# A two-layer trunk with attention woven into its projections: TensorE held in program order, VectorE released

## Chip, cores and metric

The kernel runs on one core of a Trainium2 chip. The metric is device time in microseconds. Before the change three runs took 2830.03, 2831.26 and 2836.04 us; the median is 2831.26 us.

## What is computed

A stream `x` of 2048 frames by 1024 channels passes two layers. All data are float32.

```python
# layer 0 (mixer A)
h = rms_norm(x, a_norm);  u, z = split(h @ a_w_in)
pooled = trailing_means(u, windows 2, 4, 8, 16 by channel group) - u
x = x + ((pooled @ w_group) * a_scale * silu(z)) @ a_w_out
x = x + (p[0] @ ple_w[0]) * sigmoid(x @ ple_gate_w[0])
# shared keys and values
k, v = split(rms_norm(x, kv_norm) @ w_kv);  k = rms_norm(k per head)
# layer 1 (mixer B)
q, z = split(rms_norm(x, b_norm) @ b_w_in);  q = rms_norm(q per head)
A[t,s] = beta[t,s] * prod_{s<j<t} (1 - beta[t,j]),  beta = sigmoid(q.k / 8)   # 16 heads of 64, s < t
x = x + ((A @ v) * silu(z)) @ b_w_out
x = x + (p[1] @ ple_w[1]) * sigmoid(x @ ple_gate_w[1])
```

## The kernel before

**Tiling.** The stream is cut into four chunks of 512 frames. Channels lie on the 128 partitions, eight tiles per chunk. Each float32 operand of a matmul is held as a high and a low part (a cast on ACT, then a subtraction on DVE or POOL: `split`, `put_split`), and each product is made of three matmuls, hi.hi, hi.lo, lo.hi, 128 x 128 by 512 columns. A dense output tile is 24 matmuls into one of two `psd` banks.

**Dense work** is one long generator, `stream()`. `first_part(s)` makes layer 0 for chunk s (`mixer`, `out_steps`, `gate_steps`), the gate z, and the first eight heads' q, k, v (`kvq(s, kind, 0)`); `second_part(s)` the other eight heads' q, k, v; `post(c)` is layer 1 behind attention. Each `yield` is one matmul. `marks` notes which halves are done: mark (1, 0) is `first_part(1)`.

**Weights** come through `plan`, `pump`, `unit` and `take`: nine tiles `wpair` of 512 KB turn round. In chunk 0 a unit is loaded raw (256 KB), split and written back (`once`); later it is loaded from there. A `kvq` product takes eight units and gives each back in its fourth row block (`j == 3`), so the next kind's units are loaded while the current kind ends. The weights of layer 1 behind attention (`b_w_out`, `gate_b`, `ple_b`) are split beforehand by `keep`, 36 pieces, one after each 36th dense step (`kraw`, `kp`).

**Attention** walks over 160 slots (chunk c of queries, head h, chunk kc of keys, from kc = c down to 0), four steps per slot. In step n the program issues `turn` for the step five earlier (up to four transposes of `pp` into a `psa` bank, L748; a cast to `at` on ACT, L751; a subtraction on DVE, L754), `front` (two logit matmuls into a `psl` bank, L728 and L729; a sigmoid on ACT, L731; a `TENSOR_TENSOR_SCAN` on DVE that forms the product along the keys, L736), half of the dense share (`fill`), `gather` for the step seven earlier (two output matmuls, L761 and L762), and the other half. `rate` sets the dense share: about 27 matmuls a step in chunk 0, 13 in chunk 1, 7 in chunks 2 and 3. `psa` has two banks, which the transposes of finished q and k rows (`keyed.finish`, `pst`, L552) and the norm helpers also use.

**Order.** The compiler schedules the whole program from a model of its times and may reorder each engine's instructions. `tc.keep_in_program_order` keeps the instructions so marked in the order of the program, against each other, on their engine. Before, that holds for the scans (L736) and the subtractions of `turn` (L754) on DVE, and in chunks 2 and 3 for one of six matmuls of a dense product (L225, `state["pin"]`). Everything else on TensorE is placed by the model.

**Scratch.** Finished keys and queries go to DRAM by pairs of heads, one tile `[128, 2, 512]` per pair; `load_k` reads a head's high and low rows in two DMAs, `load_q` in four.

Of the kernel before, what the change touches and what calls it, by code (L numbers as in the profile page):

```python
# [15 lines left out]
P = 128  # L16
# [3 lines left out]
NH = 16  # L20
# [16 lines left out]
def trunk_kernel(ctx, tc, x, p, a_norm, wu_t, wz_a, w_group, a_scale, a_w_out, kv_norm, w_kv,  # L37
                 k_norm, b_norm, b_w_q, b_w_z, b_q_norm, b_w_out, ple_a, ple_b, gate_a, gate_b, out):
    nc = tc.nc
    V, A, G, T = nc.vector, nc.scalar, nc.gpsimd, nc.tensor  # L40

# [32 lines left out]
    od = [[scratch(f"od{s}_{o}", [P, 2, W5]) for o in range(KT)] for s in range(NSUB)]  # L74
    qd = [[scratch(f"qd{s}_{m}", [P, 2, W5]) for m in range(NH // 2)] for s in range(NSUB)]
    kd = [[scratch(f"kd{s}_{m}", [P, 2, W5]) for m in range(NH // 2)] for s in range(NSUB)]
    vd = [[scratch(f"vd{s}_{b}", [8, P, 4, P]) for b in range(2)] for s in range(NSUB)]
# [18 lines left out]
    att = lambda nm: pool.tile([P, 2, W5], F32R, tag="at", name=nm, bufs=3)  # L96

    state = {"solo": True, "pin": False, "turn": 0, "lo": 0}

# [119 lines left out]
    def product(ps, us, acts, c0, back):  # L219
        n = len(acts)  # L220
        i = 0
        for u, kts in us:
            for e, kt in enumerate(kts):
                hi, lo = (u[:, l, e, c0 : c0 + P] for l in range(2))
                ins = T.matmul(ps, hi, acts[kt][:, 0], start=(i == 0), stop=False)  # L225
                if state["pin"] and e == 0:
                    tc.keep_in_program_order(ins)
                yield
                T.matmul(ps, hi, acts[kt][:, 1], start=False, stop=False)  # L229
                yield  # L230
                i += 1
                T.matmul(ps, lo, acts[kt][:, 0], start=False, stop=(i == n))  # L232
                if back and e == len(kts) - 1:
                    give_back()
                yield
# [251 lines left out]
    def kvq(s, kind, b):  # L487
        ck = chunk[s]
        us = take(KT)
        for j in range(4):  # L490
            tk = slice(j * P, (j + 1) * P)
            ps = dense()
            for kt in range(KT):
                u = us[kt][0]
                for xh, wh in ((0, 0), (1, 0), (0, 1)):
                    T.matmul(ps, ck["x2"][kt][:, xh, tk], u[:, wh, 0], start=(kt == 0 and xh == wh),  # L496
                             stop=(kt == KT - 1 and wh == 1))
# [35 lines left out]
    def keyed(s, kind, b, j, ps, rj):  # L533
# [15 lines left out]
        def finish(m):  # L549
# [37 lines left out]
    def gate_z(s):  # L587
# [105 lines left out]
    def load_q(c, h):  # L693
        qa, qb = qryt("qa"), qryt("qb")
        rows = qd[c][h // 2][h % 2 * HD : (h % 2 + 1) * HD]
        for l in range(2):
            nc.sync.dma_start(out=f(qa)[l * HD : (l + 1) * HD], in_=rows[:, l])
            nc.sync.dma_start(out=f(qb)[(1 - l) * HD : (2 - l) * HD], in_=rows[:, l])
        return qa, qb

    def load_k(kc, h):
        kk = keyt("kk")
        rows = kd[kc][h // 2][h % 2 * HD : (h % 2 + 1) * HD]
# [18 lines left out]
    def front(st, j):  # L722
# [10 lines left out]
        def scan():  # L733
            least = floor[:, r0:][:, ::-1] if st["diag"] else floor[:, 0:1].to_broadcast([P, w])
            tc.keep_in_program_order(
                V.tensor_tensor_scan(out=pp[:, r0:][:, ::-1], data0=pp[:, r0:][:, ::-1], data1=least,  # L736
                                     initial=1.0 if st["diag"] else st["carry"][j], op0=ALU.mult, op1=ALU.max))
            st["carry"][j] = pp[:, r0 : r0 + 1]
# [4 lines left out]
    def turn(st, kt):  # L743
        j0 = kt if st["diag"] else 0
        pt = bank("psa", "psa")
        for j in range(j0, 4):
# [5 lines left out]
        st["at"][kt] = at  # L752
        return lambda: tc.keep_in_program_order(
            V.tensor_tensor(out=at[:, 1, cs], in0=pt[:, cs], in1=f(at[:, 0, cs]), op=ALU.subtract))  # L754

# [82 lines left out]
    def fill(share):  # L838
        nonlocal owed, count
        owed += share  # L840
        while owed >= 1.0:
            next(run, None)
            owed -= 1.0
            count += 1
            if count % 36 == 0 and kept:
                keep(*kept.pop(0))

    scan = None
    for n in range(4 * len(slots) + LAG_G):
# [5 lines left out]
        if i < len(slots):  # L855
            state["pin"] = slots[i][0] >= NSUB - 2
            if j == 0 and i + 1 < len(slots):
# [15 lines left out]
    for _ in run:  # L873
        pass
    state["solo"], state["pin"] = True, False
    for _ in post(NSUB - 1):
# [65 lines left out]
```

## Time and profile before

| | |
|---|---|
| median of three runs | 2831.26 us |
| the profiled execution's own time | 2833.48 us |
| its span | 2831.7 us |
| mean granted TensorE clock | 0.986 |
| DMA, whole span | 643.43 MB, mean 227 GB/s |

Busy time counts an instruction from its start to its modelled end; matmuls overlap, so the distance from one start to the next is what a matmul takes of TensorE's time. A wait is named by the instruction that waited and the one that released it. The span starts with 354 us without attention: layer 0 and the first half of q, k, v of chunk 0. Attention of chunk 0 lasts to about 708 us, of chunk 1 to about 1416 us. From some 2760 us on only `post` of the last chunk is left.

### The profile page before, as it was taken

Reading aid. Unit: us, or ns where it says so; the run is one execution under the profiler, and the core shown is the slowest. Engines: PE = TensorE matmul, PEld = TensorE weight load, DVE = VectorE, ACT = ScalarE, POOL = GpSimd, SP = SyncE. Lnnn points to the kernel's source line nnn. Section 1 sums busy time; section 2 is a strip of 40 time slices with the busy share of each in tenths; the row PEclk is TensorE's granted clock in tenths of the full one; section 3 lists DMA queues with packets and bytes.
Section 4 is the critical chain, followed back from the end, with each engine's and each line's share of the span. In section 5 each row is a group of like instructions: output and inputs, shape, how many; then the busy total and the mean of one; then the engine's idle time right before and its main releaser. Section 6 shows DMA issues by size and latency. Waiting matters only on the chain.

```text
span 2831.7 us, 38727 instructions
## 1 busy us (share of the span) xinstructions
PE 2729.6 (96%) x13400; PEld 2250.0 (79%) x13400; DVE 1832.6 (65%) x2369; ACT 1275.0 (45%) x2496; POOL 873.3 (31%) x699
## 2 busy tenths in 40 slices
PE   7999989989999999999999999989999999999999
PEld 7888867867888888888877887868877888887767
DVE  5645446747344776655568978657667777767772
ACT  4435543445344345444444555444444444444441
POOL 1354533546533244442322434211221101111002
PEclk8999999999999999999999999999999999999999
DMA  5647899979887845668775454676586768666535
GB/s 212 223 142 277 318 340 355 325 218 302 293 289 278 255 142 174 196 226 272 254 242 163 142 158 152 225 262 206 159 276 192 249 207 263 208 194 225 169 121 185
DMA packets 300496, 643.43 MB, mean 227 GB/s; under 512 B 51206, under 2 KB 83974, under 8 KB 300300
## 3 DMA queue, kind: packets, MB, share of 16 engines
q1 hardware_dynamic: 298716, 639.63, 68.6%
q8 instruction: 106, 1.74, 0.2%
q10 hardware_dynamic: 1584, 1.33, 0.2%
q14 instruction: 90, 0.74, 0.1%
HBM read 471.43 MB, written 161.02 MB: 223 GB/s over the span
## 4 chain that ended last, share of the span: by engine, by line
PE 78%; DMA 8%; DVE 7%; ACT 2%; issue 2%; POOL 1%; SPq 1%; ACTq 0%; DVEq 0%; POOLq 0%
PE psd L496 15%; PE psd L225 11%; PE psd L229 11%; PE psd L232 11%; PE psa L748 7%; PE pso L762 4%; PE psl L729 4%; PE psl L728 3%; PE pso L761 3%; DVE pp L736 3%; PE psd L251 2%; PE psd L248 2%; PE psd L246 2%; DMA wpair<-once 2%; DVE at L754 1%
## 5 line engine op out<-in xcount | busy, mean ns | idle before, releaser
L736 DVE TENSOR_TENSOR_SCAN pp<-pp,floor 128x512 f32<-128x512 f32 (+3 forms) x640 | 779.0, 1219 | 5.2 <-ACT pp L731 4.6
L496 PE MATMUL psd<-wpair,x 128*128 128x512 f32 x2304 | 582.9, 395 | 10.0 <-ACT wpair L137 3.9
L754 DVE TENSOR_TENSOR at<-psa,at 128x512 fp32r<-128x512 f32 (+3 forms) x640 | 378.7, 595 | 312.9 <-ACT at L751 311.1
L496 PEld LDWEIGHTS psd<-wpair,x 128*128 128x128 f32 x2304 | 425.4, 189 | 98.6 <-ACT wpair L137 5.8
L751 ACT CAST at<-psa 128x512 fp32r<-128x512 f32 (+3 forms) x640 | 330.9, 523 | 378.3 <-PE psa L748 358.7
L731 ACT ACTIVATE pp<-psl 128x512 f32<-128x512 f32 (+3 forms) x640 | 333.4, 535 | 305.8 <-PE psl L729 194.8
L748 PE MATMUL psa<-ident,pp 128*128 128x128 f32 x2176 | 357.4, 276 | 45.0 <-DVE at L754 23.7
L748 PEld LDWEIGHTS psa<-ident,pp 128*128 128x128 f32 x2176 | 272.9, 141 | 132.0 <-DVE at L754 38.7
L762 PE MATMUL pso<-at,vv 128*128 128x512 f32 (+3 forms) x640 | 275.1, 430 | 0.6 <-DVE at L754 0.6
L728 PE MATMUL psl<-kk,qa 128*128 128x512 f32 (+3 forms) x640 | 244.3, 382 | 13.2 <-DMA kk<-kd 9.8
L761 PE MATMUL pso<-at,vv 128*128 128x512 f32 (+3 forms) x640 | 238.7, 374 | 7.6 <-DMA once<-kp 5.4
L729 PE MATMUL psl<-kk,qb 128*128 128x512 f32 (+3 forms) x640 | 236.0, 370 | 0.0
L225 PE MATMUL psd<-x,wpair 128*128 128x512 f32 x592 | 233.5, 394 | 0.0
L232 PE MATMUL psd<-x,wpair 128*128 128x512 f32 x592 | 232.5, 393 | 0.0
L229 PE MATMUL psd<-x,wpair 128*128 128x512 f32 x592 | 232.5, 393 | 0.0
L225 PE MATMUL psd<-xp,wpair 128*128 128x512 f32 x512 | 203.5, 398 | 0.5 <-DMA wpair<-once 0.5
L229 PE MATMUL psd<-xp,wpair 128*128 128x512 f32 x512 | 201.7, 394 | 0.0
L232 PE MATMUL psd<-xp,wpair 128*128 128x512 f32 x512 | 201.2, 394 | 0.0
L133 POOL TENSOR_TENSOR wpair<-wraw,wpair 128x512 fp32r<-128x512 f32 x98 | 139.0, 1423 | 153.6 <-ACT wpair L131 152.5
L728 PEld LDWEIGHTS psl<-kk,qa 128*128 128x128 f32 x640 | 122.8, 192 | 40.8 <-ACT pp L731 11.2
L465 POOL TENSOR_TENSOR xj<-x 128x512 f32<-128x512 f32 x64 | 106.9, 1675 | 139.6 <-DVE sg L476 131.9
L761 PEld LDWEIGHTS pso<-at,vv 128*128 128x128 f32 x640 | 122.0, 191 | 27.7 <-ACT at L751 11.0
(162 smaller groups left out, 4621.0 us busy)
## 6 DMA issues: line engine op xcount, KB each, us to landing
wpair<-once SPq DMA_DIRECT2D x384, 512.0 KB
once<-wpair SPq DMA_DIRECT2D x80, 512.0 KB
kk<-kd SPq DMA_DIRECT2D x320, 128.0 KB
vv<-vd SPq DMA_DIRECT2D x160, 256.0 KB
wpair<-wf SPq DMA_DIRECT2D x48, 512.0 KB
once<-kp SPq DMA_DIRECT2D x36, 512.0 KB
wraw<-in_a_w_out_dram SPq DMA_DIRECT2D x64, 256.0 KB
wraw<-in_gate_a_dram SPq DMA_DIRECT2D x64, 256.0 KB
```

Of the source, the lines that this page charges most:

```text
L225: ins = T.matmul(ps, hi, acts[kt][:, 0], start=(i == 0), stop=False)
L229: T.matmul(ps, hi, acts[kt][:, 1], start=False, stop=False)
L232: T.matmul(ps, lo, acts[kt][:, 0], start=False, stop=(i == n))
L496: T.matmul(ps, ck["x2"][kt][:, xh, tk], u[:, wh, 0], start=(kt == 0 and xh == wh), stop=(kt == KT - 1 and wh == 1))
L728: T.matmul(ps[:, :w], qa[:, qs], kk[:, :w], start=True, stop=False)
L729: T.matmul(ps[:, :w], qb[:, qs], kk[:, :w], start=False, stop=True)
L731: A.activation(out=pp[:, r0:], in_=ps[:, :w], func=AF.Sigmoid, scale=-1.0)
L736: V.tensor_tensor_scan(out=pp[:, r0:][:, ::-1], data0=pp[:, r0:][:, ::-1], data1=least, initial=1.0 if st["diag"] else st["carry"][j], op0 ...
L748: T.transpose(pt[:, j * P : (j + 1) * P], pp[:, r0 + kt * P : r0 + (kt + 1) * P], ident)
L754: V.tensor_tensor(out=at[:, 1, cs], in0=pt[:, cs], in1=f(at[:, 0, cs]), op=ALU.subtract))
L761: T.matmul(po[:, cs], vv[:, kt, :], at[:, 0, cs], start=(st["diag"] and kt == 0), stop=False)
L762: T.matmul(po[:, cs], vv[:, kt, :], at[:, 1, cs], start=False, stop=(st["last"] and kt == 3))
```

## The change

- Every matmul and transpose goes through a small class `T`. While `state["hold"]` is set, each is marked `keep_in_program_order`. `hold` is set when mark (0, 0) is reached, just ahead of the first attention slot, and cleared ahead of the last `post`. The pin on L225 goes.
- The scans and the subtractions of `turn` on DVE are no longer marked.
- `qd` and `kd` are stored by head, `[2, 64, 512]`: two stores per finished tile instead of one; `load_k` is one DMA instead of two, `load_q` three instead of four.
- `keep` starts only when mark (1, 0) is set.
- 60 dense matmuls instead of 24 go between the loads of the first slot and its first step.
- In `kvq`, the token norm `r2`, where it isn't there yet, comes after the first product instead of after three quarters of it. In `gate_z`, the broadcast of `r2` comes at step 20 of a product instead of 9.

```diff
-    V, A, G, T = nc.vector, nc.scalar, nc.gpsimd, nc.tensor
+    V, A, G = nc.vector, nc.scalar, nc.gpsimd
+    state = {"solo": True, "hold": False, "turn": 0, "lo": 0}
+
+    class T:
+        @staticmethod
+        def matmul(*a, **k):
+            return held_in_order(nc.tensor.matmul(*a, **k))
...
+    def held_in_order(ins):
+        return tc.keep_in_program_order(ins) if state["hold"] else ins
...
-    kd = [[scratch(f"kd{s}_{m}", [P, 2, W5]) for m in range(NH // 2)] for s in range(NSUB)]
+    kd = [[scratch(f"kd{s}_{h}", [2, HD, W5]) for h in range(NH)] for s in range(NSUB)]
...
-                ins = T.matmul(ps, hi, acts[kt][:, 0], start=(i == 0), stop=False)
-                if state["pin"] and e == 0:
-                    tc.keep_in_program_order(ins)
+                T.matmul(ps, hi, acts[kt][:, 0], start=(i == 0), stop=False)
...
-                if j == 0 and kt == 5 and "r2" not in ck:
-                    ck["r2"] = token_norm(ck["acc2"], "y")
...
+            if "r2" not in ck:
+                ck["r2"] = token_norm(ck["acc2"], "y")
...
-            nc.sync.dma_start(out=(kd if kind == "k" else qd)[s][4 * b + m], in_=f(hl))
+            for e in range(2):
+                nc.sync.dma_start(out=(kd if kind == "k" else qd)[s][8 * b + 2 * m + e].rearrange("l d n -> d l n"),
+                                  in_=f(hl)[e * HD : (e + 1) * HD])
...
-                    if first and o == 2 and i == 9:
+                    if first and o == 2 and i == 20:
...
-        for l in range(2):
-            nc.sync.dma_start(out=f(kk)[l * HD : (l + 1) * HD], in_=rows[:, l])
+        nc.sync.dma_start(out=f(kk), in_=kd[kc][h].rearrange("l d n -> (l d) n"))
...
-            tc.keep_in_program_order(
-                V.tensor_tensor_scan(out=pp[:, r0:][:, ::-1], data0=pp[:, r0:][:, ::-1], data1=least,
-                                     initial=1.0 if st["diag"] else st["carry"][j], op0=ALU.mult, op1=ALU.max))
+            V.tensor_tensor_scan(out=pp[:, r0:][:, ::-1], data0=pp[:, r0:][:, ::-1], data1=least,
+                                 initial=1.0 if st["diag"] else st["carry"][j], op0=ALU.mult, op1=ALU.max)
...
-        return lambda: tc.keep_in_program_order(
-            V.tensor_tensor(out=at[:, 1, cs], in0=pt[:, cs], in1=f(at[:, 0, cs]), op=ALU.subtract))
+        return lambda: V.tensor_tensor(out=at[:, 1, cs], in0=pt[:, cs], in1=f(at[:, 0, cs]), op=ALU.subtract)
...
-    state["solo"] = False
+    state["solo"], state["hold"] = False, True
...
-    for _ in range(24):
+    for _ in range(60):
...
-            if count % 36 == 0 and kept:
+            if count % 36 == 0 and kept and (1, 0) in marks:
```

All of TensorE's matmuls now have line 46 and its transposes line 50. The first place to look at is TensorE's order behind the second half of q, k, v of chunk 2, where attention passes from chunk 1 to chunk 2. Before (`psl` are logits, `pso` outputs, `psa` attention's transposes):

```order
L728 MATMUL psl_13973<-kk_13823,qa_13527 128x512
L729 MATMUL psl_13973<-kk_13823,qb_13528 128x512
L761 MATMUL pso_13671<-at_13821,vv_13467 128x512
L728 MATMUL psl_14018<-kk_13823,qa_13527 128x512
L729 MATMUL psl_14018<-kk_13823,qb_13528 128x512
L748 MATMUL psa_13851<-ident_60,pp_13690 128x128
L748 MATMUL psa_13851<-ident_60,pp_13723 128x128
L748 MATMUL psa_13851<-ident_60,pp_13755 128x128
L748 MATMUL psa_13851<-ident_60,pp_13793 128x128
L762 MATMUL pso_13671<-at_13821,vv_13467 128x512
L728 MATMUL psl_14042<-kk_13823,qa_13527 128x512
L729 MATMUL psl_14042<-kk_13823,qb_13528 128x512
```

The same place of the program in the changed kernel, TensorE (`psd` are dense products, `pst` transposes of finished k rows):

```order
L46 MATMUL psl_13698<-kk_13441,qa_13255 128x512
L46 MATMUL psl_13698<-kk_13441,qb_13256 128x512
L46 MATMUL psd_13648<-wpair_13539,x2_11080 128x512
L50 MATMUL pst_13706<-ident_60,qs_13300 128x128
L50 MATMUL pst_13706<-ident_60,qs_13400 128x128
L50 MATMUL pst_13706<-ident_60,qs_13474 128x128
L50 MATMUL pst_13706<-ident_60,qs_13558 128x128
L46 MATMUL psd_13648<-wpair_13544,x2_11187 128x512 x3
L46 MATMUL psd_13648<-wpair_13551,x2_11288 128x512 x3
L46 MATMUL pso_13418<-at_13609,vv_13208 128x512 x2
L46 MATMUL psd_13738<-wpair_13223,x2_10648 128x512 x3
L46 MATMUL psd_13738<-wpair_13503,x2_10674 128x512 x3
```

Three logit pairs stood within twelve instructions and no dense matmul among them; now one logit pair is followed by thirteen dense matmuls, with an output pair between.

The second place is a change from one of the q, k, v weights to the next in chunk 1, TensorE. Before (`wpair_7895`, `_8082`, `_8087`, `_8106` are the new weight's first four units):

```order
L496 MATMUL psd_8146<-wpair_8082,x2_6095 128x512 x3
L496 MATMUL psd_8146<-wpair_8087,x2_6164 128x512 x3
L496 MATMUL psd_8210<-wpair_7895,x2_6069 128x512 x3
L496 MATMUL psd_8210<-wpair_8082,x2_6095 128x512 x3
L496 MATMUL psd_8210<-wpair_8087,x2_6164 128x512 x3
L728 MATMUL psl_8400<-kk_8034,qa_8028 128x384
L729 MATMUL psl_8400<-kk_8034,qb_8029 128x384
L496 MATMUL psd_8146<-wpair_8106,x2_6258 128x512 x3
L496 MATMUL psd_8210<-wpair_8106,x2_6258 128x512 x3
```

The changed kernel at such a place (`wpair_7386`, `_7615`, `_7638`, `_7643` and so on are the units, in the order of the plan):

```order
L46 MATMUL psd_7696<-wpair_7386,x2_5927 128x512 x3
L46 MATMUL psd_7696<-wpair_7615,x2_5969 128x512 x3
L46 MATMUL psd_7696<-wpair_7638,x2_6030 128x512
L50 MATMUL psa_7704<-ident_60,pp_7309 128x128
L50 MATMUL psa_7704<-ident_60,pp_7375 128x128
L50 MATMUL psa_7704<-ident_60,pp_7441 128x128
L50 MATMUL psa_7704<-ident_60,pp_7549 128x128
L46 MATMUL psl_7711<-kk_7304,qa_7299 128x256
L46 MATMUL psl_7711<-kk_7304,qb_7300 128x256
L46 MATMUL psd_7696<-wpair_7638,x2_6030 128x512 x2
L46 MATMUL psd_7696<-wpair_7643,x2_6115 128x512 x3
L46 MATMUL psd_7696<-wpair_7648,x2_6181 128x512 x3
```

Before, a second product (`psd_8210`) was begun on the three units that were there, ahead of the first product's fourth unit; now one product runs through all its units.

More of the change, by code (lines that the diff above doesn't have):

```diff
@@ L39, in trunk_kernel, with transpose @@
     nc = tc.nc
-    V, A, G, T = nc.vector, nc.scalar, nc.gpsimd, nc.tensor
+    V, A, G = nc.vector, nc.scalar, nc.gpsimd
[4 more added lines that the diff above has]
+            return held_in_order(nc.tensor.matmul(*a, **k))
+        @staticmethod
+        def transpose(*a, **k):
+            return held_in_order(nc.tensor.transpose(*a, **k))
+    def held_in_order(ins):
+        return tc.keep_in_program_order(ins) if state["hold"] else ins
     cp = ctx.enter_context(tc.tile_pool(name="cp", bufs=1))
@@ L74, in trunk_kernel @@
     od = [[scratch(f"od{s}_{o}", [P, 2, W5]) for o in range(KT)] for s in range(NSUB)]
-    qd = [[scratch(f"qd{s}_{m}", [P, 2, W5]) for m in range(NH // 2)] for s in range(NSUB)]
-    kd = [[scratch(f"kd{s}_{m}", [P, 2, W5]) for m in range(NH // 2)] for s in range(NSUB)]
+    qd = [[scratch(f"qd{s}_{h}", [2, HD, W5]) for h in range(NH)] for s in range(NSUB)]
+    kd = [[scratch(f"kd{s}_{h}", [2, HD, W5]) for h in range(NH)] for s in range(NSUB)]
     vd = [[scratch(f"vd{s}_{b}", [8, P, 4, P]) for b in range(2)] for s in range(NSUB)]
@@ L96, in trunk_kernel @@
     att = lambda nm: pool.tile([P, 2, W5], F32R, tag="at", name=nm, bufs=3)
-    state = {"solo": True, "pin": False, "turn": 0, "lo": 0}
     def bank(tag, nm):
@@ L694, in load_q @@
         qa, qb = qryt("qa"), qryt("qb")
-        rows = qd[c][h // 2][h % 2 * HD : (h % 2 + 1) * HD]
+        nc.sync.dma_start(out=f(qa), in_=qd[c][h].rearrange("l d n -> (l d) n"))
         for l in range(2):
-            nc.sync.dma_start(out=f(qa)[l * HD : (l + 1) * HD], in_=rows[:, l])
-            nc.sync.dma_start(out=f(qb)[(1 - l) * HD : (2 - l) * HD], in_=rows[:, l])
+            nc.sync.dma_start(out=f(qb)[(1 - l) * HD : (2 - l) * HD], in_=qd[c][h][l])
         return qa, qb
@@ L702, in load_k @@
         kk = keyt("kk")
-        rows = kd[kc][h // 2][h % 2 * HD : (h % 2 + 1) * HD]
-        for l in range(2):
-            nc.sync.dma_start(out=f(kk)[l * HD : (l + 1) * HD], in_=rows[:, l])
+        nc.sync.dma_start(out=f(kk), in_=kd[kc][h].rearrange("l d n -> (l d) n"))
         return kk
@@ L855, in trunk_kernel @@
         if i < len(slots):
-            state["pin"] = slots[i][0] >= NSUB - 2
             if j == 0 and i + 1 < len(slots):
@@ L874, in trunk_kernel @@
         pass
-    state["solo"], state["pin"] = True, False
+    state["solo"], state["hold"] = True, False
     for _ in post(NSUB - 1):
```

## Prediction

> **What bounds the kernel now.** I read the page's first lines, then the busy time by stage, then TensorE's waits, then the timeline at the worst waits.
>
> ```profile
> span 2831.7 us, 38727 instructions
> PE 2729.6 (96%) x13400; PEld 2250.0 (79%) x13400; DVE 1832.6 (65%) x2369; ACT 1275.0 (45%) x2496; POOL 873.3 (31%) x699
> ```
>
> TensorE is the bound; the rest of the span, 102 us, is its idle time. What can be won is idle time, and time at half clock. The stages (columns: stretch, length, busy time of PE, PEld, DVE, ACT, POOL, then granted clock, DMA share, GB/s) say where these lie:
>
> ```profile
> 0.00:354.00 354.00, 339.11 (x1589) 286.56 (x1590) 193.94 (x338) 162.70 (x300) 142.62 (x128) 0.97 0.66 234
> 354.00:708.00 354.00, 323.32 (x1491) 264.04 (x1489) 210.50 (x260) 153.67 (x304) 167.58 (x136) 0.97 0.91 308
> 708.00:1416.00 708.00, 701.85 (x3468) 581.38 (x3467) 416.88 (x541) 316.84 (x633) 279.60 (x226) 1.00 0.73 238
> 1416.00:2620.00 1204.00, 1165.56 (x5901) 959.11 (x5900) 887.52 (x1079) 566.67 (x1116) 259.52 (x193) 0.99 0.65 207
> 2620.00:2832.00 212.00, 199.78 (x957) 158.90 (x956) 123.74 (x153) 75.12 (x144) 24.00 (x17) 0.98 0.50 157
> ```
>
> Idle time plus clock loss (length times one minus the clock) per stage: first, before attention, 14.9 + 10.6, which the change doesn't touch; second, attention of chunk 0, 30.7 + 10.6 = 41 us; third, 6; fourth, 38.4 + 12 = 50; last, 12.2 + 4.2 = 16. So 91 of the removable 113 us lie in the second and fourth. TensorE's waits by cause:
>
> ```profile
> PE psa L748 <- DVE at L754: 23.7, 35, 2.1
> PE psd L281 <- ACT uh L268: 14.7, 2, 7.8
> PE psa L748 <- DVE pp L736: 13.8, 9, 4.5
> PE psl L728 <- DMA kk<-kd: 9.8, 3, 5.3
> PE pso L761 <- DMA once<-kp: 5.4, 1, 5.4
> PE psa L748 <- DVE hl L120: 4.6, 2, 3.4
> PE psd L496 <- ACT wpair L137: 3.9, 4, 1.6
> ```
>
> Nearly all are attention instructions (L748, L728, L761) that wait for something a few us old. The dense matmuls that could have covered them had been put elsewhere. The fourth stage at its start shows it:
>
> ```profile
> 1430.26 0.60 PE L748 MATMUL psa<-ident,pp 128*128 128x128 f32 x4
> 1430.61 0.48 PE L761 MATMUL pso<-at,vv 128*128 128x512 f32 x1
> 1432.16 0.66 PE L552 MATMUL pst<-ident,qs 128*128 128x128 f32 x4 [1.07 <-DVE at L754]
> ...
> 1436.92 0.39 PE L728 MATMUL psl<-kk,qa 128*128 128x512 f32 x1
> 1437.15 0.40 PE L729 MATMUL psl<-kk,qb 128*128 128x512 f32 x1
> 1437.53 0.49 PE L761 MATMUL pso<-at,vv 128*128 128x512 f32 x1
> 1441.45 0.88 PE L748 MATMUL psa<-ident,pp 128*128 128x128 f32 x3 [3.43 <-DVE hl L120]
> 1443.27 0.66 PE L748 MATMUL psa<-ident,pp 128*128 128x128 f32 x2 [0.94 <-DVE at L754]
> ```
>
> From 1430 to 1443 us not one dense matmul (psd) runs: attention and its transposes stand back to back, so a psa bank is asked for again before ScalarE and VectorE have emptied it. (Start to start, a 512-wide matmul takes 1437.15 - 1436.92 = 0.23 us, four transposes 0.35.) In the second stage the cause is different:
>
> ```profile
> 630.26 0.62 ACT L119 CAST ple<-pin 128x512 fp32r<-128x512 f32 x1 [2.53 <-DMA pin<-in_p_dram]
> ...
> 630.91 0.69 DVE L120 TENSOR_TENSOR ple<-pin,ple 128x512 fp32r<-128x512 f32 x1 [2.46 <-ACT ple L119]
> 631.52 1.22 DVE L736 TENSOR_TENSOR_SCAN pp<-pp,floor 128x512 f32<-128x512 f32 x1
> ...
> 632.79 1.11 PE L748 MATMUL psa<-ident,pp 128*128 128x128 f32 x4 [4.52 <-DVE pp L736]
> ...
> 634.34 0.63 PE L229 MATMUL psd<-ple,wpair 128*128 128x512 f32 x1
> 634.77 0.63 PE L232 MATMUL psd<-ple,wpair 128*128 128x512 f32 x1
> ```
>
> A load is late (DMA share 0.91), ACT's cast waits for it, the split on DVE for ACT, the scan stands behind the split, and TensorE behind the scan: 4.52 us. After that the pace is 0.43 us per matmul: half clock. The Trainium skill (TensorE: Matmul & The Clock Gate, "The HAM clock gate") halves the clock after an idle window of about 3.4 us and restores it after a busy one; the 4.52 us wait agrees, and by that rule waits under 3.4 us cost only themselves.
>
> **The change, part by part.**
>
> *TensorE in program order, fourth stage.* A step in program order is four transposes, two logit matmuls, half of the dense share, two output matmuls, the other half. What a transposition's bank needs before reuse, and what the output matmul needs before it starts, is one cast and one subtraction, with at most a scan ahead of them:
>
> ```profile
> L751 ACT CAST at<-psa 128x512 fp32r<-128x512 f32 x448 | 260.7, 587 | 301.1 <-PE psa L748 288.4 <-PE pso L762 7.0 <-DVE at L754 1.5
> L754 DVE TENSOR_TENSOR at<-psa,at 128x512 fp32r<-128x512 f32 x448 | 301.3, 676 | 258.1 <-ACT at L751 257.1
> L736 DVE TENSOR_TENSOR_SCAN pp<-pp,floor 128x512 f32<-128x512 f32 x448 | 620.5, 1386 | 4.9 <-ACT pp L731 4.3
> ```
>
> 0.59 + 0.68 = 1.3 us, with a scan 2.7. I counted in both orders, with the spacings above, how much TensorE work lies in between. psa banks reused within 2.5 us, from chunk 2 up to the last dense-free stretch: 55 before, none now. Output matmuls within 2 us of their transposition, whole kernel: 83 before, 1 now. Stretches over 2 us without a dense matmul: 64 before (247 us), 5 now (49 us, nearly all at the very end). Keys come at least 10 us after their buffer is free (4.5 us before), the very end apart. So the causes L754, hl, L736 and kk go in this stage. VectorE could still be late by itself: its busy share is 887.52/1204 = 0.74. I leave 8 of the 50 us: **-42**; bounds 0 and -50.
>
> *Second stage.* Splitting b weights (36 pieces of 256 KB read, 512 KB written, 28 MB in all) moves behind mark (1, 0), to the third stage, whose DMA share is 0.73. The second stage moved 308 GB/s x 354 us = 109 MB, so it loses up to a quarter of its traffic, and the casts that wait for these loads. That removes the 5.4 us at once<-kp and most waits of the scan kind. Against it: program order takes away what TensorE did at a change of the q, k, v weights. Before, it ran two products in turn on the units already there; now all eight units are needed in a row, 3 x 0.23 = 0.69 us apart. A unit's buffer is free 24 matmuls, 5.5 us, before its successor's turn, with a step's attention (0.35 + 4 x 0.23 = 1.3 us) some 6.7. What landing takes under load (from the chain of waits and the timeline):
>
> ```profile
> 820.52 6.02 DMA wpair<-once
> ...
> 1235.24 9.16 DMA wpair<-once
> ...
> 826.58 0.98 PE L496 MATMUL psd<-wpair,x 128*128 128x512 f32 x3 [1.52 <-DMA wpair<-once]
> ...
> 780.00:830.00 50.00, 48.06 (x246) 39.94 (x245) 24.29 (x35) 21.83 (x45) 19.84 (x17) 1.00 0.85 288
> ```
>
> Unit tiles whose buffer comes free less than 8 us before use: 26 before, 69 now. Seven units of 0.524 MB at 288 GB/s take 12.7 us; the last is due 6.7 + 6 x 0.8 = 11.5 us after the first buffer is free. That is a wait of 1 to 3 us per change. Two changes lie in this stage, and their units still pass through a cast and a split (the 3.9 us at wpair L137), so I take 4 us each, and leave 7 us of the rest: 41 becomes 15, **-26**; bounds +20 and -41.
>
> *Third stage.* Eleven further changes have short leads, six of 6 to 7.5 us and five near 8, and the b weights' traffic now lies here. I take the low end for the six and next to nothing for the five: 6 x 1 + 5 x 0.2 = **+7**; bounds 0 and +33 (11 x 3). The page's best slice moved 355 GB/s; at that rate seven units take 10.3 us. The Trainium skill (DMA: Bandwidth & Descriptors, "Where 436 GB/s comes from") gives the port ceiling as 435 GB/s and HBM's share as about 358: at the ceiling this estimate would be 8.4 us, the waits and this term would vanish and the sum would be 7 us lower. No slice here is above 355.
>
> *The end.* The last attention steps have no dense work in either kernel (30 steps, 43 us of issue in both orders), but the stream runs dry 36 matmuls earlier, since 60 instead of 24 go ahead of attention (36 x 0.23 = 8 us moved, none added). VectorE sets the pace there:
>
> ```profile
> 2683.00:2755.00 72.00, 36.75 (x30) 0.95 0.34 107
> 2683.00:2755.00 72.00, 21.08 (x34) 0.95 0.34 107
> ```
>
> (scans, then subtractions): 1.23 + 0.62 = 1.85 us a step against TensorE's 1.3. In strict order the scan of a slot's last row has as little as 1.7 us of issue before it is read. **+4**; bounds -5 and +16 (30 x 0.55).
>
> *VectorE's order free*: scans and subtractions may now swap with dense work. Bounds: the 13.8 us of scan waits gone, or doubled; both are inside the stage bounds; I take 0, nearest the group's 4.9 us of idle before scans. *Keys and queries by head*: 160 + 64 loads fewer, 64 stores more, all on SP, which nothing on TensorE's list names except kk (9.8 us, counted above): 0; if the two stores came late, the cover is the half chunk between projection and attention. *r2 after the whole product, rb2 at step 20 instead of 9*: 11 x 0.23 = 2.5 us more cover for the chain through POOL: 0.
>
> Sum against the profiled execution: 2833.5 - 42 - 26 + 7 + 4 = 2776.5. That execution is 2.2 us above the median of the runs (2831.3), so 2774, rounded 2775.
>
> **The rivals.**
>
> *VectorE takes over (half the gain).* Where chunk 3's mixer runs beside chunk 2's attention, it is nearly full:
>
> ```profile
> 1558.00:1628.00 70.00, 68.73 (x351) 56.51 (x350) 63.26 (x74) 37.91 (x75) 29.03 (x24) 1.00 0.47 140
> ```
>
> 63.26/70 = 0.90, and yet TensorE lost only 1.3 us in that slice; that speaks against it. If half of the 42 and 26 stays: 2774 + 34 = 2808.
>
> *Slower: the weight changes.* Thirteen changes have the short leads. I charged 15 us. If the seven units arrive later than I think (the 9.16 us landing is the row for it), each change waits 4.5 us and, as at 632.79, runs about 11 matmuls at half pace (11 x 0.2 = 2.2): 13 x 6.7 = 87 us, 2774 + 72 = 2846. It decides from (57 + 15)/13 = 5.5 us a change. Against it: waits of 1.5 us on these weights today, at leads of 6.3 us and more. By the clock rule cited above, waits that stay under 3.4 us leave this case impossible, since 13 x 3.4 = 44.
>
> *No difference.* The compiler's order might not bind, but the printed orders differ as described, so only gains and losses that cancel remain: 2831.
>
> **How the numbers follow.** Forecast 0.62; half the gain 0.22; no difference 0.05; weight changes 0.11. The forecast's own range is 2735 (2831 less all 91 us, and 5 won at the end) to 2798 (a third of the 68 us stays); with the half gain and the 16 us that the end may cost on top of it (2808 + 16), the range is 2735 to 2824. A measurement here tells about 0.2% from no change (5.7 us; the three runs spread over 6). Faster 0.84, same 0.05, slower 0.11.
>
> **What would show it.** Right: the fourth stage's idle time under 10 us, L748's waits for L754 near zero before the last 140 us, the second stage's clock near 1.00. The new waits stand at psd for wpair at the changes of q, k, v, each 1 to 3 us. Wrong: waits over 3.4 us there with a clock under 0.97 between 354 and 1416 us; or L748 still waiting for L754 and L736 in the fourth stage with VectorE over 0.85 busy; or a last stage with over 25 us idle.

## The result and the profile after

The changed kernel takes 2836.6 us (median of 20 runs) where the kernel before takes 2832.5 us on the same chip: ratio 1.0015, 95% interval 1.0008 to 1.0022. That lies inside the 0.2% which count as no difference. The forecast of 2775 us and its range, 2735 to 2824, are missed. The page of the changed kernel begins like this:

```profile
span 2832.9 us, 38130 instructions
...
PE 2733.4 (96%) x13400; PEld 2246.7 (79%) x13400; DVE 1840.4 (65%) x2369; ACT 1271.2 (45%) x2496; POOL 870.4 (31%) x699
```

Span and busy times are within a few us of before. By the page's head, then, nothing happened. The stages say otherwise (columns: stretch, length, busy time of PE, PEld, DVE, ACT, POOL, then granted clock, DMA share, GB/s):

```profile
354.00:708.00 354.00, 327.67 (x1507) 266.61 (x1506) 190.15 (x250) 138.39 (x271) 139.98 (x117) 0.96 0.73 239
708.00:1416.00 708.00, 672.88 (x3241) 546.05 (x3239) 413.03 (x521) 312.77 (x628) 293.91 (x236) 0.98 0.78 259
1416.00:2620.00 1204.00, 1194.04 (x6098) 986.47 (x6097) 913.22 (x1104) 579.57 (x1150) 267.40 (x202) 1.00 0.66 215
2620.00:2833.00 213.00, 198.99 (x975) 160.55 (x973) 130.10 (x158) 78.24 (x150) 27.01 (x19) 0.99 0.49 163
```

By the prediction's measure, idle time plus length times one minus the clock, the stages lose this much in us. (The clock has two digits, which leaves about 2, 4 and 6 us open in the three.)

| | second | third | fourth | last |
|---|---|---|---|---|
| before | 30.7 + 10.6 = 41 | 6 | 38.4 + 12 = 50 | 16 |
| after | 26.3 + 14.2 = 41 | 35.1 + 14.2 = 49 | 10.0 + 0 = 10 | 14.0 + 2.1 = 16 |

The fourth stage gained 40 us, and the third gave 43 back. TensorE's waits in the changed kernel, whole span, and behind them the first of these in the third stage alone (708 to 1416 us):

```profile
PE psd L46 <- DMA wpair<-once: 29.1, 28, 7.2
PE psd L46 <- ACT uh L277: 14.2, 2, 8.1
PE psd L46 <- ACT wpair L148: 13.6, 5, 6.1
PE psd L46 <- DVE xr L449: 7.5, 2, 4.2
PE psa L50 <- DVE pp L743: 6.6, 9, 2.0
PE psa L50 <- DVE at L760: 5.5, 9, 1.2
```

```profile
PE psd L46 <- DMA wpair<-once: 24.0, 24, 7.2
```

The wait of transposes for the subtraction fell from 23.7 to 5.5 us, that for the scan from 13.8 to 6.6. The list is now headed by dense matmuls that wait for weight units, 29.1 us in 28 waits (before, 3.2 us in 3), 24.0 us of them in the third stage. Another 13.6 us (before, 3.9) go to units that ACT still casts; all of these lie in the second stage, the longest 6.1 us. The start of the fourth stage, for comparison with the dense-free stretch of before (timeline of TensorE):

```profile
1430.06 0.60 PE L50 MATMUL psa<-ident,pp 128*128 128x128 f32 x4
1430.41 0.36 PE L46 MATMUL psl<-kk,qa 128*128 128x256 f32 x1
1430.61 0.28 PE L46 MATMUL psl<-kk,qb 128*128 128x256 f32 x1
1430.73 1.53 PE L46 MATMUL psd<-wpair,x 128*128 128x512 f32 x6
1432.10 0.40 PE L46 MATMUL pso<-at,vv 128*128 128x256 f32 x2
1432.33 1.79 PE L46 MATMUL psd<-wpair,x 128*128 128x512 f32 x7
```

Thirteen dense matmuls stand in a step, and nothing waits. What the order costs shows at a change of the q, k, v weights in chunk 1, the one whose order stands ahead of the prediction, first on TensorE and then on SP's queue (start, duration, engine, line, tile, count):

```profile
816.65 0.39 PE L46 MATMUL psd<-wpair,x 128*128 128x512 f32 x1
...
823.20 0.94 PE L46 MATMUL psd<-wpair,x 128*128 128x512 f32 x3
831.34 2.30 PE L46 MATMUL psd<-wpair,x 128*128 128x512 f32 x4 [7.20 <-DMA wpair<-once]
```

```profile
818.17 0.58 SPq L713 DMA_DIRECT2D kk<-kd  x1
...
819.32 3.33 SPq L571 DMA_DIRECT2D kd<-hl  x4
822.75 0.70 SPq L540 DMA_DIRECT2D vd<-vv  x1
823.50 3.36 SPq L523 DMA_DIRECT2D vs<-vr  x2
826.91 0.41 SPq L530 DMA_DIRECT2D ve<-vr  x1
827.43 4.06 SPq L156 DMA_DIRECT2D wpair<-once  x8
```

At 823.20 stand the three matmuls of the new weight's first unit; for the second TensorE waits 7.20 us. The matmul at 816.65 is the first on the old weight's second unit in its last row block, so a buffer was free by then. The loads were not slow to land so much as late to be issued: SP was issuing without a gap from 818 us on, and the units' turn came at 827.43. The stretch in and behind the wait runs at half clock:

```profile
828.00:832.00 4.00, 0.66 (x2) 0.56 (x3) 0.69 (x1) 0.62 (x1) 1.26 (x1) 0.50 0.85 294
```

The Trainium skill (TensorE: Matmul & The Clock Gate, "The HAM clock gate") halves the clock after an idle window of about 3.4 us; a wait of 7.20 us with a clock of 0.50 agrees.

### The profile page after: what moved, and what is told of

Its sections match the earlier page's. It is cut to its first block, busy times and chain, and to the rows that moved or that the text cites. A ratio compares the mean times of both kernels' runs of the same rounds, so it can differ in the third digit from the quotient of the medians.

```text
span 2832.9 us, 38130 instructions
## 1 busy us (share of the span) xinstructions
PE 2733.4 (96%) x13400; PEld 2246.7 (79%) x13400; DVE 1840.4 (65%) x2369; ACT 1271.2 (45%) x2496; POOL 870.4 (31%) x699
## 4 chain that ended last, share of the span: by engine, by line
PE 79%; DMA 8%; DVE 5%; SPq 2%; issue 2%; ACT 2%; POOL 2%; ACTq 0%; DVEq 0%; POOLq 0%
PE psd L46 55%; PE psl L46 8%; PE pso L46 7%; PE psa L50 7%; DMA wpair<-once 3%; DVE pp L743 2%; DVE at L760 1%; DMA wraw<-in_b_w_q_dram 1%; PE pst L50 1%; DMA xin<-in_x_dram 1%; DMA vs<-vr 1%; POOL wpair L144 1%; PE pst L46 1%; SPq L523 1%; DMA kraw<-in_b_w_out_dram 1%
## 5 line engine op out<-in xcount | busy, mean ns | idle before, releaser
L46 PE MATMUL psd<-x,wpair 128*128 128x512 f32 x2304 | 599.3, 393 | 3.5 <-ACT sg L481 3.5
L46 PEld LDWEIGHTS psd<-x,wpair 128*128 128x128 f32 x2304 | 427.0, 188 | 92.5 <-ACT sg L481 4.6
L46 PE MATMUL psd<-xp,wpair 128*128 128x512 f32 x1536 | 391.8, 396 | 6.4 <-DMA wpair<-once 6.4
L46 PE MATMUL pso<-at,vv 128*128 128x512 f32 (+3 forms) x1280 | 361.5, 364 | 0.2 <-DVE at L760 0.2
L46 PEld LDWEIGHTS psd<-xp,wpair 128*128 128x128 f32 x1536 | 287.4, 190 | 66.3 <-DMA wpair<-once 7.7
L46 PEld LDWEIGHTS pso<-at,vv 128*128 128x128 f32 x1280 | 240.7, 189 | 54.0 <-DVE at L760 0.5
L46 PE MATMUL psd<-og,wpair 128*128 128x512 f32 x744 | 202.6, 395 | 2.0 <-DVE os L773 2.0
L46 PE MATMUL psd<-mp,wpair 128*128 128x512 f32 x768 | 196.9, 398 | 7.5 <-DVE xr L449 7.5
L46 PEld LDWEIGHTS psd<-mp,wpair 128*128 128x128 f32 x768 | 145.0, 192 | 38.2 <-DVE xr L449 8.3
L46 PEld LDWEIGHTS psd<-og,wpair 128*128 128x128 f32 x744 | 137.5, 188 | 31.5 <-DVE os L773 2.6
```

Source lines behind the costliest of these rows:

```text
L46: return held_in_order(nc.tensor.matmul(*a, **k))
```

## The experiments

The theory after the result: program order of TensorE does in the fourth stage what was forecast, and loses it again at the weight changes of the second and third stage. Rivals: the new place of the b weights, the storage by head, VectorE's freed order. No kernel below leaves anything out of the computation. Ratios are to the kernel before, with their 95% intervals.

### Program order only from chunk 2 on

```diff
-    state["solo"], state["hold"] = False, True
+    state["solo"] = False
...
         x_ = rate(i)
+        state["hold"] = slots[min(i, len(slots) - 1)][0] >= NSUB - 2
```

> The changed kernel, but TensorE is held in program order only while chunks 2 and 3 attend; chunks 0 and 1 are placed by the compiler as before. Weight-change theory (in chunks 0 and 1 strict order uses up new q, k, v units faster than they land): the fourth stage keeps its gain (idle about 10 us instead of 38) and the second and third lose most of their 43 + 14 us of waits at wpair, so about 2800 us. Queue theory (the two stores per key or query tile hold up SP's queue, whatever TensorE's order): waits at wpair stay, about 2820. Moved-traffic theory (b weights split in the third stage): third stage idle stays above 20 us, about 2820.

Measured: 2805.3 us, ratio 0.9898 (0.9882 to 0.9913).

```profile
354.00:708.00 354.00, 339.00 (x1565) 275.84 (x1564) 196.96 (x260) 142.54 (x282) 149.47 (x121) 0.98 0.75 250
708.00:1416.00 708.00, 687.48 (x3367) 566.74 (x3366) 420.81 (x537) 322.39 (x649) 304.37 (x241) 0.99 0.79 266
1416.00:2620.00 1204.00, 1194.38 (x6093) 988.49 (x6092) 922.42 (x1109) 577.79 (x1144) 261.27 (x195) 0.99 0.65 214
```

The second stage loses 15 + 7 = 22 us instead of 41, the third 20.5 + 7 = 28 instead of 49, and the idle time of the fourth is as low as in the changed kernel (9.6 us; its clock reads 0.99 instead of 1.00). The waits for units from `once` fell from 29.1 to 7.0 us. So program order in chunks 0 and 1 costs (1.0015 - 0.9898) x 2832.5 = 33 us in this kernel, and the fourth stage keeps its idle gain without it. The 20.5 us of idle time that stay in the third stage are the sign that the moved-traffic theory named (above 20), though its time of 2820 us wasn't reached.

### Keys and queries by pairs of heads again

```diff
-            for e in range(2):
-                nc.sync.dma_start(out=(kd if kind == "k" else qd)[s][8 * b + 2 * m + e].rearrange("l d n -> d l n"),
-                                  in_=f(hl)[e * HD : (e + 1) * HD])
+            nc.sync.dma_start(out=(kd if kind == "k" else qd)[s][4 * b + m], in_=f(hl))
```

(with the tiles and the loads of before)

> The changed kernel with keys and queries stored and loaded by pairs of heads again, one store per tile. Queue theory: SP's issue time for these stores falls by about 59 us, the unit loads behind them go out earlier, waits at wpair halve, about 2815 us. Weight-change theory: no difference to the changed kernel beyond 5 us, 2836. Moved-traffic theory: 2836.

Measured: 2826.8 us, ratio 0.9977 (0.9966 to 0.9989): 11 us faster than the changed kernel, so storage by head has a price.

```profile
354.00:708.00 354.00, 332.31 (x1525) 270.76 (x1524) 193.17 (x251) 139.12 (x272) 142.45 (x119) 0.96 0.74 239
708.00:1416.00 708.00, 677.12 (x3266) 550.58 (x3265) 417.88 (x526) 316.62 (x637) 291.99 (x235) 0.98 0.78 259
```

4.6 us of TensorE's idle time went in the second stage and 4.2 in the third. The time lies between the 2815 us of the queue theory and the 2836 of the other two. The waits for loaded units fell from 29.1 to 25.0 us, and those for units that ACT casts from 13.6 to 8.3.

### The b weights split as early as before

```diff
-            if count % 36 == 0 and kept and (1, 0) in marks:
+            if count % 36 == 0 and kept:
```

> The changed kernel with the b weights split from the start of attention again. Moved-traffic theory: the third stage's idle time falls from 35 us below 15, the second's rises by what it gains from the move (some 10 to 20 us), total 2825 to 2836. Weight-change theory: the third stage keeps at least 25 us of its 35, the second gets worse, total 2840 to 2855.

Measured: 2836.1 us, ratio 1.0008 (0.9998 to 1.0017), no difference from the changed kernel. But the stages differ:

```profile
354.00:708.00 354.00, 318.62 (x1421) 255.36 (x1420) 205.24 (x253) 147.85 (x285) 158.34 (x128) 0.93 0.86 291
708.00:1416.00 708.00, 686.10 (x3338) 559.82 (x3337) 409.06 (x521) 307.19 (x616) 272.91 (x225) 0.99 0.71 233
```

The second stage loses 35.4 + 24.8 = 60 us instead of 41, the third 21.9 + 7.1 = 29 instead of 49. The move is worth 20 us to one stage and costs the other 20. Both theories missed their sign: the third stage's idle time, 21.9 us, is neither below 15 nor at 25 or more.

### Row blocks of q, k, v in pairs

`kvq` runs two of its four row blocks at a time, on both `psd` banks, so that the eight units of a weight are needed over 48 matmuls instead of 24 (the first two and the last two by one row block after the other, the four between by both at once; the steps that finish q and k rows move to matching places):

```diff
+    ORDER = ([(0, 0), (0, 1), (1, 0), (1, 1)] + [(r, kt) for kt in range(2, 6) for r in range(2)]
+             + [(0, 6), (0, 7), (1, 6), (1, 7)])
...
-        for j in range(4):
-            tk = slice(j * P, (j + 1) * P)
-            ps = dense()
-            for kt in range(KT):
+        for j0 in (0, 2):
+            pss = [dense(), dense()]
+            for n, (r, kt) in enumerate(ORDER):
```

> The changed kernel with kvq's four row blocks taken in two pairs, so that a unit is read by six matmuls at a time: the time between a buffer's last read and its successor's first use goes from about 6 to about 11 us, and all else of the change stays. Weight-change theory: waits at wpair in the second and third stage nearly vanish (29 + 14 us below 10), clock back to 0.99 there, about 2790 us; a few us go to the psd banks, which change hands faster. Queue theory: the unit loads still stand behind the stores, at most half of it goes, about 2815. Moved-traffic theory: 2825.

Measured: 2806.5 us, ratio 0.9909 (0.9892 to 0.9925). TensorE's wait for units and the same two stages:

```profile
PE psd L46 <- DMA wpair<-once: 5.9, 3, 2.5
```

```profile
354.00:708.00 354.00, 334.58 (x1568) 275.31 (x1567) 194.64 (x254) 142.32 (x277) 149.63 (x122) 0.98 0.75 248
708.00:1416.00 708.00, 680.46 (x3322) 558.68 (x3322) 426.82 (x540) 321.94 (x647) 303.52 (x239) 0.99 0.79 265
```

Waits for units fell from 29.1 to 5.9 us with TensorE in program order everywhere, and the time by (1.0015 - 0.9909) x 2832.5 = 30 us. So much of what program order costs comes from eight units demanded three matmuls apart, 0.524 MB each 0.69 us or 760 GB/s without attention in between, where such stretches moved some 290 GB/s. Pairs ask for half of that over the eight units. The 2790 us of the weight-change theory were not reached; other waits came up, the longest at the start of attention, where the first logits wait 10.5 us for a key load (2.9 in the changed kernel).

### Combinations

With keys and queries by pairs of heads again, and program order only from chunk 2 on:

> Program order on TensorE from chunk 2 on only, and the old layout. As above: with the units' lead given back by the compiler's order, the layout is worth nothing more if it acts only through late units, 2803 to 2808 us; about 2796 if it costs by itself.

Measured: 2792.2 us, ratio 0.9856 (0.9839 to 0.9872), below both figures: the storage by head costs here too.

With keys and queries by pairs of heads again, and row blocks in pairs:

> Both repairs at once: row blocks in pairs, and keys and queries stored and loaded by pairs of heads. If the stores act only by making unit loads late (weight-change theory with the queue as its cause), the longer lead already covers them and little is left to win: 2800 to 2806 us. If they cost by themselves, the 10 us of the layout run come on top: about 2796.

Measured: 2799.6 us, ratio 0.9883 (0.9868 to 0.9898). All three together:

> Pairs of row blocks, the old layout, and program order on TensorE from chunk 2 on only. If strict order in chunks 0 and 1 still costs after the pairs have given the units their lead (other waits: kk, xr, wraw), this is faster than pairs_layout by 5 us or more, about 2790; if the units were all that strict order cost, the two are equal within 4 us.

Measured: 2786.1 us, ratio 0.9834 (0.9819 to 0.9849). The storage is worth 12 us with the one (0.9898 - 0.9856) and 7 with the other, each to within some 6 us; pairs and late order share most of what they win, as they should if both remove the same waits. They don't share all of it: with pairs, program order in chunks 0 and 1 still costs (0.9883 - 0.9834) x 2832.5 = 14 us, where it costs (0.9977 - 0.9856) x 2832.5 = 34 without them. The second stage has most of that, first with order everywhere, then with order from chunk 2 on:

```profile
354.00:708.00 354.00, 338.63 (x1587) 278.85 (x1587) 195.61 (x257) 142.78 (x279) 149.95 (x123) 0.98 0.76 248
```

```profile
354.00:708.00 354.00, 342.48 (x1615) 280.95 (x1614) 196.64 (x259) 143.19 (x284) 153.77 (x125) 1.00 0.77 256
```

That is 15.4 + 7 = 22 us against 11.5. The late units are not all that strict order costs; a 7.8 us wait for a key load stands in the first of these kernels and not in the second.

### VectorE's scans and subtractions kept, with TensorE in order

```diff
-            V.tensor_tensor_scan(...
+            tc.keep_in_program_order(V.tensor_tensor_scan(...
...
-        return lambda: V.tensor_tensor(...
+        return lambda: tc.keep_in_program_order(V.tensor_tensor(...
```

> The changed kernel with the scans and the subtractions on VectorE kept in program order again. If the released order helped nor hurt (as I priced it), 2836 within 4 us; if VectorE's freedom is part of what the fourth stage won, TensorE's waits there come back by 5 us or more, 2842.

Measured: 2961.4 us, ratio 1.0454 (1.0433 to 1.0475). This was the largest surprise: 124 us slower than the changed kernel, where 2842 was the worst expected. TensorE's waits, then a stretch of DVE's timeline and POOL's at the same place:

```profile
PE psa L50 <- DVE pp L744: 65.6, 23, 16.6
...
PE psa L50 <- DVE at L762: 43.9, 19, 12.9
```

```profile
1520.01 0.69 DVE L539 TENSOR_TENSOR vv<-vs,vv 128x512 fp32r<-128x512 f32 x1 [6.14 <-ACT vv L538]
1520.62 0.68 DVE L762 TENSOR_TENSOR at<-psa,at 128x512 fp32r<-128x512 f32 x1
1536.56 0.69 DVE L539 TENSOR_TENSOR vv<-vs,vv 128x512 fp32r<-128x512 f32 x1 [15.26 <-ACT vv L538]
1537.17 1.22 DVE L744 TENSOR_TENSOR_SCAN pp<-pp,floor 128x512 f32<-128x512 f32 x1
```

```profile
1534.61 1.26 POOL L535 TENSOR_TENSOR vs<-vs,vr 128x512 f32<-128x512 f32 x1 [15.29 <-DMA vs<-vr]
```

DVE stands 15.26 us at the split of a value row (L539). That waits for ACT's cast, the cast for POOL's difference, and POOL for the load of the shifted rows `vs`. Behind it stand the scans, and behind them TensorE, whose longest wait is 16.6 us. This row is the last of four, and it stands two places behind the third. In the changed kernel the same two rows stand fifteen places apart on DVE, with scans and subtractions between them:

```profile
1477.96 0.69 DVE L539 TENSOR_TENSOR vv<-vs,vv 128x512 fp32r<-128x512 f32 x1 [5.11 <-ACT vv L538]
...
1494.25 1.14 DVE L539 TENSOR_TENSOR vv<-vs,vv 128x512 fp32r<-128x512 f32 x1 [2.00 <-ACT vv L538]
```

There DVE waits only 2.00 us at the last row; the work between covers the load.

### The same, with the value split on POOL

```diff
-        A.copy(out=vv[:, :, 0, :], in_=vs)
-        V.tensor_tensor(out=vv[:, :, 1, :], in0=vs, in1=f(vv[:, :, 0, :]), op=ALU.subtract)
+        G.tensor_copy(out=vv[:, :, 0, :], in_=vs)
+        G.tensor_tensor(out=vv[:, :, 1, :], in0=vs, in1=f(vv[:, :, 0, :]), op=ALU.subtract)
```

> The changed kernel with the scans and the subtractions of turn in program order again, and the value rows' split (vv: cast on ACT, subtraction on DVE) moved to POOL, which forms their difference anyway. Theory: the 125 us that the fixed order on VectorE cost (2961) came from one instruction, the subtraction of the last value row, which that order puts some 13 rows earlier, so that the scans behind it wait 10 to 17 us for the load of shifted rows (vs<-vr). With the split on POOL nothing on ACT or DVE waits for that load: 2845 to 2880, and no wait of psa over 6 us. Rival: the fixed order of scans and subtractions among themselves and against the dense work costs by itself: still over 2920, with the long psa waits at other releasers.

Measured: 2884.0 us, ratio 1.0181 (1.0168 to 1.0195); TensorE's waits:

```profile
PE psa L50 <- DVE pp L744: 23.2, 19, 5.0
PE psa L50 <- DVE at L762: 22.1, 22, 3.0
```

The long waits are gone, and 77 of the 124 us; the number is 4 us above the range that the theory gave. So the value rows are the larger part. A rest of 47 us stays, in kind as the rival had it though far below its 2920: 45 us of waits for scans and subtractions, against 12 in the changed kernel. That the fixed order itself causes this rest is likely, but not shown: the same run also gives POOL 81 us more to do (951.5 us busy against 870.4).

### Only VectorE's order freed

The kernel before, with the marks on scans and subtractions taken away.

> The kernel before, with the scans and the subtractions of turn no longer marked, and nothing else changed. Theory: without TensorE in program order the compiler's model binds both engines together, and VectorE's release is worth at most the 13.8 us of scan waits: 2815 to 2833. Rival: the release by itself is worth what it is worth in strict order, tens of us: under 2800. Third: it is worse, since TensorE's and VectorE's orders part: over 2840.

Measured: 2813.5 us, ratio 0.9929 (0.9916 to 0.9943), a little below the range that the theory gave. Its fourth stage:

```profile
1416.00:2620.00 1204.00, 1179.75 (x5990) 975.15 (x5989) 906.32 (x1089) 578.62 (x1127) 262.85 (x194) 0.99 0.66 210
```

24.3 us idle against 38.4. So half of the 28 us of idle time that left the fourth stage in the changed kernel can be had without program order on TensorE.

### The stores of keys and queries from POOL's queue

```diff
-                nc.sync.dma_start(out=(kd if kind == "k" else qd)...
+                nc.gpsimd.dma_start(out=(kd if kind == "k" else qd)...
```

> The changed kernel, with the 128 stores of keys and queries by head issued from POOL's queue instead of SP's; nothing else changed. Theory: storing by head costs some 10 us because the issue of these stores (0.6 to 0.7 us each) stands on SP's queue ahead of the unit loads at a change of weights; off SP's queue this goes, 2822 to 2829, and waits of psd for wpair fall below after's 29 us. Rival: the cost lies in the transfers themselves (twice as many stores, packets of 2 KB on half of the partitions), or in landing order, whoever issues them: 2833 to 2840.

Measured: 2836.6 us, ratio 1.0014 (1.0003 to 1.0025), as the changed kernel. The theory fell: the waits for units only went from 29.1 to 26.1 us.

```profile
PE psd L46 <- DMA wpair<-once: 26.1, 30, 4.4
```

At the change shown above one unit was issued at 820.72 now, and the next still only at 826.80, behind the load of `vs`:

```profile
820.72 1.09 SPq L156 DMA_DIRECT2D wpair<-once  x1
821.91 4.32 SPq L523 DMA_DIRECT2D vs<-vr  x2
...
826.80 1.34 SPq L156 DMA_DIRECT2D wpair<-once  x3
```

Why storage by head costs some 10 us stays open. The time that SP takes to issue these stores doesn't explain it, unless the 81 us that POOL is busy longer in this run (951.0 against 870.4) cost as much as SP saves; that was not separated.

### The best orders found

Pairs, the storage of before, and program order from chunk 1 on instead of chunk 2:

> The changed kernel with row blocks of q, k, v in pairs, keys and queries stored by pairs of heads, and TensorE in program order from chunk 1's attention on instead of chunk 2's. If program order costs only in the second stage (chunk 0's attention, where weights are still split), this is at or under the 2786 of program order from chunk 2: 2775 to 2786. If it costs also in the third stage (six weight changes with short leads, now with paired row blocks), between 2786 and the 2800 of program order everywhere: 2788 to 2800.

Measured: 2785.4 us, ratio 0.9832 (0.9818 to 0.9845), the same as from chunk 2 on to within some 6 us: with paired row blocks no price of program order in the third stage can be told, and the 14 us found above belong to chunk 0's attention. The version from chunk 2 on with the value split on POOL:

> The best kernel so far (paired row blocks, keys and queries stored by pairs of heads, TensorE in program order from chunk 2 on: 2786), with the value rows' split moved to POOL as in dve_kept_pool. If value loads still stall ACT and DVE in front of attention in chunks 2 and 3: 2770 to 2782. If VectorE's free order already hides them, or POOL becomes late: 2784 to 2795.

Measured: 2783.0 us, ratio 0.9826 (0.9813 to 0.984); no difference can be told. The version from chunk 1 on with that split:

> Paired row blocks, keys and queries stored by pairs of heads, TensorE in program order from chunk 1 on (2785.4), with the value rows' split on POOL. If the value loads still stalled ACT and DVE: 2775 to 2783. If the free order of VectorE hides them: 2783 to 2790.

Measured: 2778.4 us, ratio 0.9811 (0.9794 to 0.9829). It beats the kernel before by 54 us and the changed one by 58. Whether the split on POOL has a part in it is not settled, since its interval overlaps with that of the same order without it.

## Why the prediction was wrong

On one path from the kernel before to the changed one, the time is a sum of four steps that almost cancel. By ratios, times 2832.5 us, each uncertain by some 4 to 6 us:

| from | to | us |
|---|---|---|
| before | VectorE's order freed | -20 |
| that | TensorE in order from chunk 2 on, b weights later, the small edits | -21 |
| that | keys and queries by head | +12 |
| that | TensorE in order in chunks 0 and 1 too | +33 |

Together +4: gains were there, though smaller than forecast, and so were losses of the same size. Another path would price the steps otherwise: VectorE's release is worth 20 us as the first step and 124 as the last. Point by point:

- *Fourth stage, -42.* Measured -40. Size and place were right, the size partly by luck, for the whole was put down to TensorE's order: VectorE's release alone takes 14 of those 28 us of idle time, and TensorE's order without it makes the stage worse (in the kernel with both kept, 1204 - 1126.77 = 77 us idle, clock 0.97):

```profile
1416.00:2620.00 1204.00, 1126.77 (x5633) 924.95 (x5634) 833.50 (x1021) 538.99 (x1063) 257.81 (x197) 0.97 0.60 197
```

- *Second stage, -26.* Measured 0. The traffic left as said (DMA share 0.91 to 0.73), and by the kernel with the b weights early that is worth 20 us here. But the two weight changes with the units that are still cast were charged 4 us each, 8 together. The waits for cast units alone rose from 3.9 to 13.6 us, and order from chunk 2 on takes 18 us out of this stage.
- *Third stage, +7.* Measured +43; this is the step that failed most. It held two errors. The b weights' traffic was seen to arrive here and was given no price, beside a DMA share of 0.73: the run with the b weights early takes 20 us out of this stage, as much as the second stage gained. And the eleven weight changes were charged 6 x 1 + 5 x 0.2: order from chunk 2 on takes 22 us out of this stage. No run has both, so how far the two overlap isn't known. The mechanism was named, with its leads of 6 to 8 us; the size was wrong. The waits for loaded units alone came to 24.0 us here, 2.2 us a change, inside the 1 to 3 us that the prediction itself had worked out and of which it charged the low end and less; the clock, 0.98, cost some 14 us on top. That working took the rate at which seven units land, as if their loads were issued when their buffers came free. At the change shown they were issued some 10 us later (816.65 to 827.43), behind other DMAs on SP's queue.
- *Keys and queries by head, 0.* Measured +7 to +12. The reason given was that nothing on TensorE's list named these transfers. With the old storage it was the waits for weight units that fell, so transfers that no wait names can still cost.
- *VectorE's order free, 0.* Measured -20 by itself and -124 with TensorE in strict order, against bounds of plus or minus 13.8. The bound was taken from the waits of scans in the kernel before. With TensorE in order and VectorE fixed a late value row stops the chain, and no wait in the trace of before shows that: there a TensorE order made by the same model stood beside it (that this is the reason wasn't tested).
- *The end, +4.* Measured 0 (16 us lost in both). The places of `r2` and `rb2`, and the pin on L225, were not tried by themselves.
- *The rivals.* "No difference" came, in the way it was described, by gains and losses that cancel, at a chance of 0.05. "Slower: the weight changes" had the right mechanism; even if all 33 us of program order are put down to the 13 changes, that is 2.5 us each, below its 5.5 and above the 15/13 = 1.2 that the forecast charged. "VectorE takes over" did not come: waits of transposes for DVE went down.

The sign named beforehand for a wrong forecast was waits over 3.4 us at psd for wpair with a clock under 0.97 between 354 and 1416 us. The second stage shows it: a wait of 6.1 us for a cast unit, one of 3.8 us for a loaded one, and a clock of 0.96 where about 1.00 was forecast. The wait of 7.20 us lies in the third stage, whose clock read 0.98. Of the signs of a right forecast the fourth stage's idle time came about (10.0 us where under 10 was named), and so did the place of the new waits; the second stage's clock did not.

## What to carry to other kernels

When an engine is put into program order, count for each stream that it consumes how fast the program asks for it (here 0.524 MB in 0.69 us) beside how fast it lands, and look on the issuing queue for what stands ahead of its loads. A fixed order on one engine may only be judged together with the order of the engines that feed it: the same marks on VectorE cost 20 us with TensorE placed by the compiler and 124 us with TensorE in program order. Work that is moved out of a full stage has a price in the stage that gets it, even if that stage's averages show room.

## What was not expected of the hardware

Storing a tile of queries (or keys) by head, 64 partitions into two blocks each, holds SP's queue longer than storing a pair of heads in one contiguous piece, though it has half of the bytes. Issue times of the kernel before and of the changed kernel (minimum, median, maximum in ns):

```profile
L561 SPq DMA_DIRECT2D qd<-hl x32: 319/334/1374, 334.5 to 2072.2; - x32
```

```profile
L571 SPq DMA_DIRECT2D qd<-hl x64: 574/610/1868, 335.3 to 2070.8; - x64
```

Yet the same stores from POOL, 592 ns each at the least, left the time where it was.
